# Which engine issues 120 stores of token sums in a decoder trunk's MLP

## The chip, the cores and the metric

The kernel runs on one core of a Trainium2 chip. The metric is the device time of one execution in microseconds (us), as the median of several runs. The core has a matrix engine (TensorE, PE in the profile, with its weight loads as PEld) and three engines for elementwise work: VectorE (DVE), ScalarE (ACT) and GpSimd (POOL). SyncE (SP) computes nothing here: its queue issues DMA transfers between on-chip memory and DRAM. Each engine works through its own list of instructions in order; a DMA is an instruction in the list of the engine that issues it, and the transfer then goes on by itself. Engines wait for each other, and for DMAs, through semaphores.

## What is computed

One layer of a decoder trunk for 2048 tokens of width 1024, in float32: a mixer (four retention heads beside a causal pooling mixer), cross-attention into 256 memory tokens, and a gated MLP, each behind an RMS norm and with a residual, and a last norm. The change lies in the MLP and in what prepares its operands:

```python
def conv_glu_ffn(h, w_up, conv_w, conv_b, w_down):
    a = h @ w_up                                  # 1024 -> 2 x 2816
    ...
    c = conv_w[0] * a2 + conv_w[1] * a1 + conv_w[2] * a + conv_b
    gate, val = jnp.split(c, 2, axis=-1)
    return (jax.nn.silu(gate) * val) @ w_down     # 2816 -> 1024
```

Here `a1` and `a2` are `a` shifted by one and two tokens.

## The kernel before

**Products.** Every float32 product is made from three matmul passes (L241 to L243): each operand is split in a high part and a low part, and high by high, high by low and low by high are added up. A high part is a copy (ACT, L955 for tokens, L1006 for weights), a low part is the difference (L216, on POOL or DVE). The MLP's two big products are done in blocks of two by two with seven block products in place of eight (the scheme of Strassen and Winograd). That needs, besides the blocks themselves, four sums of blocks on the weights' side and four on the tokens' side.

**Tokens' sums.** The tokens are held feature by token, as tiles of 128 features by 512 tokens (256 KB). They come in two blocks of 1024 tokens. Four tiles, two features by two halves of a block's tokens, give seven operand tiles. `sums_of` (L963) makes the four sums, all on POOL, in two steps: `t = b22 - b12`, `b12 = b11 - b12`, then `b11 = b11 + t`, `b21 = b11 - b21`. The seven tiles are written to DRAM, to `Hd` for the up product and to `Gd` for the down product: the originals as numbers 0, 3, 5 (and 7), the sums as 4, 1, 2 and 6. All these stores go through `send` (L972). `combining` (L944) loads an operand tile again later (`T<-Hd`, `T<-Gd`, L948) and splits it.

**Three places make them.** `first_tiles` (L1456) takes the first block's tiles, during the attention of the last block, near 1070 to 1120 us. It goes through four groups: load four tiles (`T<-Xd`, L1453), scale them (DVE, L225), sum, store, free. `later_tiles` (L1468) does the same with the second block's, step by step within the first block's up products (the first up round), at 1300 to 1380 us. Both use `normed_tiles` (L1429), with its store of the originals at L1438 and of the sums at L1445. For the down product, `Up.conv` makes a gated column of the up product's result; as soon as two columns that belong together are there, `pair` (L1099) loads the earlier one's tiles again (L1105, L1106), has POOL sum them with the later one's and stores the sums in `keep` (L1109). This happens 11 times in each of the two blocks.

**Places.** `T` is a set of ten places for tiles of 512 tokens (later re-cut to eleven, and two more named `state` and `consts` in the profile). Whatever takes a place waits until the last use of it is over, a store's landing included. `R` holds ten raw weight tiles, and seven pairs (`Q` and the end of `G`) hold split weights that wait for PE; `Z` holds the up product's results and gated columns, and the down product's sums.

**Order.** The Python code gives the program order by hand: `run` (L1324) walks over the products, a clock counts them, and `after(n, f)` puts a step n products later. From that order the framework's scheduler makes each engine's list with its own model of the instructions' times, so that a change of an instruction's engine can also shift instructions on other engines. An engine's list runs strictly in order: a store in SP's list that waits for POOL holds back the loads behind it.

**Weights' sums.** POOL issues DMAs already before the MLP: `weight_sums` (L903) adds blocks of the weights in DRAM by accumulating DMAs (`Ud<-w_up`, `Ud<-Ud` and the same for `Dd`, L915 to L922), 136 of them, between 47 and 936 us.

Of the kernel before, what the change touches and what calls it, by code (L numbers as in the profile page):

```python
# [21 lines left out]
SUB = 512  # L22
# [97 lines left out]
def trunk(ctx, tc, xT, memT, pos, w_qkgu, w_v, wkv, wqT, wo, wout_r, wout_p, poolT, w_up, w_dn, vecs, consts, outT):  # L120
    nc = tc.nc
    pe, act, dve, pool, sp = nc.tensor, nc.scalar, nc.vector, nc.gpsimd, nc.sync
# [42 lines left out]
    def cst(n):  # L165
        nonlocal o
        o += n
        return cs_t[:, o - n : o]

    ident, one = cst(P), cst(1)  # L170
# [8 lines left out]
    Hd = drp.tile([NB, KT // 2, 7, P, SUB], F32, tag="Hd", name="Hd")  # L179
# [7 lines left out]
    t = TT.take()  # L187
# [27 lines left out]
    def tt(eng, out, a, b, op):  # L215
        return eng.tensor_tensor(out=out, in0=a, in1=b, op=op)  # L216
# [7 lines left out]
    def stt(out, a, s, b, op0=ALU.mult, op1=ALU.add):  # L224
        dve.scalar_tensor_tensor(out=out, in0=a, scalar=s, in1=b, op0=op0, op1=op1)  # L225
# [737 lines left out]
    def sums_of(b11, b12, b21, b22, t):  # L963

        tt(pool, t, b22, b12, ALU.subtract)
        tt(pool, b12, b11, b12, ALU.subtract)
        yield
        tt(pool, b11, b11, t, ALU.add)
        tt(pool, b21, b11, b21, ALU.subtract)
        yield  # L970

    def send(to, aps):  # L972
        for i, a in aps.items():
            sp.dma_start(to[i], a)

    def in_turn(gens):

# [48 lines left out]
    class Up(Member):  # L1026
# [29 lines left out]
        def conv(self, g):  # L1056

            f = self.f + g * NF
            src = self.val if g else self.gate
            a = src.f[:, EDGE - 2 :]  # L1060

            def one():
                until_room(CC, 1)
                self.c[g] = CC.take()
                if self.b:
                    pool.tensor_copy(a[:, :2], halo[:, f])
                else:
                    pool.tensor_copy(halo[:, f], a[:, T:])
                act.activation(self.c[g].f, a[:, 2:], AF.Identity, bias=cb[:, f : f + 1], scale=cw[2][:, f : f + 1])  # L1069

            def two():
                c = self.c[g].f
                stt(c, a[:, 1 : T + 1], cw[1][:, f : f + 1], c)

            def three():
                c = self.c[g].f
                stt(c, a[:, :T], cw[0][:, f : f + 1], c)
                src.free()

            def four():  # L1080
                act.activation(self.c[0].f, self.c[0].f, AF.Silu)

            def five():
                tt(dve, self.c[1].f, self.c[1].f, self.c[0].f, ALU.mult)
                self.c[0].free()

                c = self.c[1]
                one, two = (c.f[:, h * SUB : (h + 1) * SUB] for h in ((1, 0) if self.b == NB - 1 else (0, 1)))
                at, second = halves[self.f]
                to = Gd[self.b, at]  # L1090

                def store():
                    send(to, {3: one, 5: two} if second else {0: one, 7: two})
                    if second:
                        pair()
                    else:
                        c.free()

                def pair():  # L1099
                    if TT.room() < 3:  # L1100
                        after(1, pair)
                        return
                    x = [TT.take() for _ in range(3)]
                    b11, b12, t = (r.f[:, :SUB] for r in x)
                    sp.dma_start(b12, to[7])  # L1105
                    sp.dma_start(b11, to[0])  # L1106
                    todo = sums_of(b11, b12, one, two, t)

                    def keep():  # L1109
                        send(to, {4: t, 1: b12, 2: b11, 6: one})  # L1110
                        for r in (*x, c):
                            r.free()

                    after(2, lambda: next(todo))
                    after(3, lambda: next(todo))
                    after(5, keep)

                after(2, store)

            return [one, two, three] + ([five] if g else [four])  # L1120
# [174 lines left out]
    def after(n, f):  # L1295

        waiting.append((clock[0] + n, f))

    def until_room(places, n):

        for _ in range(99):
            if places.room() >= n:
                return
            w = min(waiting, key=lambda w: w[0])
            waiting.remove(w)
            w[1]()
        assert False, "no room"
# [121 lines left out]
    def normed_tiles(b, j, q, rb):  # L1429

        for i, v in enumerate(q):
            n, s = j + 4 * (i // 2), i % 2
            stt(v, v, ffng[:, n : n + 1], rb[s].f[:, :SUB], ALU.mult, ALU.mult)
        if j == KT // 2 - 1:
            for r in rb:
                r.free()
        yield
        send(Hd[b, j], {0: q[0], 5: q[3], 3: q[2]})  # L1438
        t = TT.take()
        todo = sums_of(*q, t.f[:, :SUB])  # L1440
        next(todo)
        yield
        next(todo)
        yield
        send(Hd[b, j], {4: t.f[:, :SUB], 1: q[1], 2: q[0], 6: q[2]})  # L1445
        t.free()
        yield

# [7 lines left out]
    def first_tiles(own):  # L1456

        rb = [TT.take() for _ in range(NS)]
        spread(own[0], [r.f[:, :SUB] for r in rb], late=True)
        yield  # L1460
        for j in range(KT // 2):
            x = fetch_tiles(0, j)
            yield
            yield from normed_tiles(0, j, [r.f[:, :SUB] for r in x], rb)
            for r in x:
                r.free()

    def later_tiles(b, j, rb):  # L1468

        x = fetch_tiles(b, j)  # L1470
        steps = normed_tiles(b, j, [r.f[:, :SUB] for r in x], rb)

        def step():
            if next(steps, True) is None:
                after(2, step)
            else:
                for r in x:
                    r.free()

        after(2, step)  # L1480
# [246 lines left out]
```

## Time and profile before

| | |
|---|---|
| Runs shown | 2500.76, 2502.49, 2505.65 us |
| Median | 2502.49 us |
| The profiled execution | 2506.72 us (span of its instructions 2504.9 us, clock of PE 0.992 of full speed) |
| DMA, mean over the span | 474 MB, 189 GB/s |
| `T<-Xd` loads, by SP | 53 of 256 KB, 4.6 us to landing |
| `T<-Gd` loads, by SP | 168 of 256 KB, 4.1 us |
| SP waiting at a store for POOL (`T` and `Z`) | 67.6 + 17.5 us |

The profile is of one execution. Its page gives, for each engine, how long it was busy; a window gives the same for a stretch of time; a wait tells what an engine stood still for, in us in total, times and longest us. A group's row has the line of the code, the engine, the operation, output and input, then busy time and mean ns, and the idle time before it with what ended that. `POOL T L216` means: an instruction of POOL, of line 216, that writes `T`.

### The profile page before, as it was taken

To read this page: it belongs to the slowest core of one execution; us is meant where nothing else is said; L and a number is where in the kernel's file an instruction comes from. 1 tells how busy PE (TensorE), PEld (TensorE's weight loads), DVE (VectorE), ACT (ScalarE), POOL (GpSimd) and SP (SyncE) were. 2 spreads that over 40 slices of the span, in tenths; PEclk is the share of its full clock that TensorE was granted. 3 is DMA by queue.
4 is the path that set the end of the run, shared out by engine and by line. 5 is a ranking of instruction groups with operands and counts; after the bars stand their busy time and mean duration, and the time that the engine had idled before them with its cause. 6 is when DMAs were issued, how large, how long until landed. Compare 5 with 4: busy or idle time off the path is not lost.

```text
span 2504.9 us, 33172 instructions
## 1 busy us (share of the span) xinstructions
PE 2442.7 (98%) x11390; PEld 2037.7 (81%) x11390; DVE 1666.9 (67%) x2574; ACT 1216.1 (49%) x2163; POOL 652.4 (26%) x579
## 2 busy tenths in 40 slices
PE   6999999999999999999999999999999999999997
PEld 6888887788788888888887888878888887888885
DVE  8646566564635675574678776886677586867875
ACT  6333423343321223434654555665555576666663
POOL 1010122100121120030237352553335154222322
PEclk9999999999999999999999999999999999999998
DMA  8363888715766764366567564755556468768951
GB/s 318 89 168 110 244 191 233 234 40 181 227 152 145 159 158 149 111 221 220 167 205 270 166 203 153 236 192 165 160 160 213 136 220 287 250 185 280 346 164 68
DMA packets 257177, 474.28 MB, mean 189 GB/s; under 512 B 26864, under 2 KB 56176, under 8 KB 257008
## 3 DMA queue, kind: packets, MB, share of 16 engines
q1 hardware_dynamic: 212336, 408.18, 49.0%
q0 software_dynamic: 19584, 34.61, 8.9%
q10 hardware_dynamic: 25088, 29.37, 3.4%
q8 instruction: 89, 1.46, 0.2%
q14 instruction: 80, 0.66, 0.1%
HBM read 370.87 MB, written 170.39 MB: 216 GB/s over the span
## 4 chain that ended last, share of the span: by engine, by line
PE 78%; DMA 8%; DVE 6%; issue 3%; POOL 2%; ACT 2%; SPq 0%; POOLq 0%; ACTq 0%; DVEq 0%
PE mm L241 25%; PE mm L242 24%; PE mm L243 24%; POOL T L216 1%; DVE Z L216 1%; DMA T<-Xd 1%; DVE Z L225 1%; DVE G L216 1%; DMA T<-xT 1%; DVE Q L216 1%; DVE T L216 1%; DMA T<-Gd 1%; POOL Z L216 1%; PE aux L749 1%; DMA R<-VWd 0%
## 5 line engine op out<-in xcount | busy, mean ns | idle before, releaser
L241 PE MATMUL mm<-G,Q 128*128 128x512 f32 (+1 forms) x1888 | 728.1, 386 | 21.8 <-ACT Q L233 11.1
L243 PE MATMUL mm<-G,Q 128*128 128x512 f32 (+1 forms) x1888 | 725.9, 385 | 4.4 <-DVE Q L216 4.2
L242 PE MATMUL mm<-G,Q 128*128 128x512 f32 (+1 forms) x1888 | 725.7, 385 | 0.7 <-DVE G L216 0.7
L241 PE MATMUL mm<-G 128*128 128x512 f32 (+1 forms) x1380 | 532.1, 387 | 10.0 <-DVE Z L216 6.3
L242 PE MATMUL mm<-G 128*128 128x512 f32 (+1 forms) x1380 | 531.7, 386 | 0.0
L243 PE MATMUL mm<-G 128*128 128x512 f32 (+1 forms) x1380 | 531.1, 385 | 0.0
L241 PEld LDWEIGHTS mm<-G,Q 128*128 128x128 f32 x1888 | 357.8, 190 | 91.1 <-ACT Q L233 11.8
L243 PEld LDWEIGHTS mm<-G,Q 128*128 128x128 f32 x1888 | 357.7, 190 | 74.3 <-DVE Q L216 5.9
L242 PEld LDWEIGHTS mm<-G,Q 128*128 128x128 f32 x1888 | 358.0, 190 | 69.4 <-DVE G L216 1.6
L225 DVE SCALAR_TENSOR_TENSOR Z<-Z,vecs 128x1024 f32<-128x1024 f32 x176 | 276.3, 1572 | 153.5 <-ACT Z L1069 145.3
L241 PEld LDWEIGHTS mm<-G 128*128 128x128 f32 x1380 | 260.4, 189 | 64.5 <-DVE Z L216 8.0
L243 PEld LDWEIGHTS mm<-G 128*128 128x128 f32 x1380 | 260.2, 189 | 51.8
L242 PEld LDWEIGHTS mm<-G 128*128 128x128 f32 x1380 | 260.1, 188 | 51.5
L1006 ACT ACTIVATE G<-R 128x512 fp32r<-128x512 f32 (+1 forms) x272 | 166.5, 615 | 197.8 <-PE mm L242 178.6
L216 DVE TENSOR_TENSOR Z<-Z,mm 128x512 f32<-128x512 f32 x284 | 192.8, 679 | 78.2 <-PE mm L243 78.0
L216 DVE TENSOR_TENSOR Q<-R,Q 128x512 fp32r<-128x512 f32 x199 | 148.6, 748 | 143.4 <-ACT Q L233 138.9
L216 POOL TENSOR_TENSOR G<-R,G 128x512 fp32r<-128x512 f32 (+1 forms) x100 | 141.9, 1420 | 376.2 <-ACT G L1006 290.9
L233 ACT ACTIVATE Q<-R 128x512 fp32r<-128x512 f32 x150 | 93.8, 627 | 234.8 <-PE mm L242 187.3
L1006 ACT ACTIVATE Q<-R 128x512 fp32r<-128x512 f32 (+1 forms) x204 | 125.0, 613 | 90.9 <-PE mm L242 73.5
L216 DVE TENSOR_TENSOR G<-R,G 128x512 fp32r<-128x512 f32 (+1 forms) x168 | 131.5, 794 | 46.7 <-ACT G L233 38.0
L216 DVE TENSOR_TENSOR G<-T,G 128x512 fp32r<-128x512 f32 (+1 forms) x168 | 125.4, 758 | 53.9 <-ACT G L955 40.7
L940 ACT ACTIVATE aux<-R 128x512 f32<-128x512 f32 (+1 forms) x184 | 105.8, 576 | 95.8 <-DVE Q L216 52.9
(222 smaller groups left out, 2911.4 us busy)
## 6 DMA issues: line engine op xcount, KB each, us to landing
R<-Ud SPq DMA_DIRECT2D x176, 256.0 KB, 2.7
T<-Gd SPq DMA_DIRECT2D x168, 256.0 KB, 4.1
R<-w_up SPq DMA_DIRECT2D x132, 256.0 KB, 3.1
Gd<-Z SPq DMA_DIRECT2D x110, 256.0 KB, 2.4
Ud<-w_up SPq DMA_DIRECT2D x88, 256.0 KB, 5.9
R<-w_qkgu SPq DMA_DIRECT2D x32, 512.0 KB, 4.4
R<-Dd SPq DMA_DIRECT2D x64, 256.0 KB, 4.0
Gd<-T SPq DMA_DIRECT2D x56, 256.0 KB, 3.1
```

The costliest lines, as they stand in the source:

```text
L216: return eng.tensor_tensor(out=out, in0=a, in1=b, op=op)
L225: dve.scalar_tensor_tensor(out=out, in0=a, scalar=s, in1=b, op0=op0, op1=op1)
L233: act.activation(hi, src, AF.Copy)
L241: pe.matmul(ps, lh, rh, start=start, stop=False, skip_group_check=more)
L242: pe.matmul(ps, lh, rl, start=False, stop=False, skip_group_check=more)
L243: pe.matmul(ps, ll, rh, start=False, stop=stop, skip_group_check=more)
L749: pe.matmul(col(self.kv, c), col(self.kn.f, c), self.ch(v, c, h * T), start=True, stop=True)
L940: act.activation(t, x, AF.Copy)
L1006: act.activation(p2[:, 0, :w], self.raw[i].f[:, :w], AF.Copy)
```

## The change

`send` gets an argument that says which engine issues the stores, SP where nothing is given. The two calls that store the four sums pass POOL, the engine that has made them. The stores of the originals (0, 3, 5, 7) and all loads stay with SP. 32 stores to `Hd` and 88 to `Gd` change their engine.

```diff
-    def send(to, aps):
+    def send(to, aps, by=sp):
         for i, a in aps.items():
-            sp.dma_start(to[i], a)
+            by.dma_start(to[i], a)
...
                     def keep():
-                        send(to, {4: t, 1: b12, 2: b11, 6: one})
+                        send(to, {4: t, 1: b12, 2: b11, 6: one}, pool)
...
         next(todo)
         yield
-        send(Hd[b, j], {4: t.f[:, :SUB], 1: q[1], 2: q[0], 6: q[2]})
+        send(Hd[b, j], {4: t.f[:, :SUB], 1: q[1], 2: q[0], 6: q[2]}, pool)
         t.free()
```

## The prediction

> **What bounds the kernel now.** I read the page's busy times first.
>
> ```profile
> span 2504.9 us, 33172 instructions
> ...
> PE 2442.7 (98%) x11390; PEld 2037.7 (81%) x11390; DVE 1666.9 (67%) x2574; ACT 1216.1 (49%) x2163; POOL 652.4 (26%) x579
> ```
>
> PE is idle for 2504.9 − 2442.7 = 62 us in all, so only work that PE waits for, or comes to wait for, can move the time. The moved stores run between 1069 and about 2085 us. Next I read busy times by window there (columns: PE, PEld, DVE, ACT, POOL busy, then PE's clock, DMA share, GB/s), and the waits of PE in three stretches (1060 to 1130, 1290 to 1400, 2000 to 2120).
>
> ```profile
> 1060.00:1125.00 65.00, 64.80 (x307) 53.22 (x306) 47.21 (x85) 22.39 (x59) 22.41 (x17) 1.00 0.57 200
> 1290.00:1390.00 100.00, 94.20 (x406) 76.81 (x405) 79.12 (x77) 49.07 (x75) 67.23 (x47) 0.98 0.75 255
> ...
> 1350.00:1370.00 20.00, 16.81 (x69) 13.50 (x68) 17.04 (x15) 9.29 (x15) 16.28 (x12) 0.93 0.76 265
> 1700.00:1800.00 100.00, 100.00 (x443) 82.84 (x442) 67.05 (x67) 56.98 (x84) 40.27 (x34) 1.00 0.52 163
> 2050.00:2100.00 50.00, 46.69 (x200) 38.19 (x199) 35.22 (x41) 33.37 (x63) 24.79 (x18) 0.97 0.75 250
> ```
> ```profile
> PE aux L850 <- DVE T L220: 0.2, 1, 0.2
> ```
> ```profile
> PE mm L241 <- DVE Z L216: 5.8, 3, 3.2
> ```
> ```profile
> PE mm L241 <- ACT G L955: 3.3, 1, 3.3
> PE mm L241 <- DVE Z L216: 0.5, 1, 0.5
> ```
>
> So there are three places to price: the attention's end (PE full, POOL a third busy), a stretch of the MLP's first up round (1290 to 1390: POOL already busy 67 of 100 us, PE loses 5.8), and the passage from the up to the down products near 2080 (PE loses 3.3). In the steady stretch from 1700 PE has no gap.
>
> An idle us costs more than itself, since the clock dips after it: 443 matmuls in 100 us are 0.226 us each, so the 69 of 1350 to 1370 should take 15.6 us and took 16.81 beside 3.2 us idle, and the 200 of 2050 to 2100 should take 45.1 and took 46.69 beside 3.3. I charge 1.4 us for each us of new or removed idle time.
>
> **What the change moves.** 120 stores of 256 KB (32 to `Hd`, 88 to `Gd`) leave SP's queue and stand in POOL's stream behind the sums that make them. No byte and no sum is added. What a store costs on either side:
>
> ```profile
> Hd<-T SPq DMA_DIRECT2D x49, 256.0 KB, 2.4
> ...
> Ud<-Ud POOLq DMA_DIRECT2D x44, 256.0 KB, 6.1
> ```
> ```profile
> L974 SPq DMA_DIRECT2D Hd<-T x49: 319/320/752, 1069.0 to 1376.1; - x49
> ```
> ```profile
> L216 POOL TENSOR_TENSOR T<-T 128x512 f32<-128x512 f32 x57 | 88.8, 1559 | 170.8 <-DVE T L225 166.7 <-DMA Hd<-T 1.6
> ...
> L916 POOL DMA_DIRECT2D Ud<-w_up x22 | 21.5, 978 | 8.3 <-DMA Ud<-w_up 6.1 <-issue 1.9 <-DVE G L216 0.3
> L915 POOL DMA_DIRECT2D Ud<-w_up x22 | 19.8, 900 | 384.8 <-DMA Ud<-w_up 384.8
> L919 POOL DMA_DIRECT2D Ud<-Ud x22 | 18.3, 832 | 87.5 <-DMA Ud<-w_up 84.6 <-DVE sm L222 2.9
> ```
> ```profile
> L922 POOL DMA_DIRECT2D Ud<-Ud x22: 802/812/1127, 63.1 to 714.9; - x22
> ...
> DMA to landing us min/median/max: 3.7/5.3/7.4
> ```
>
> SP issues a store in 0.32 us. The trace has no plain store by POOL; its nearest row is the accumulating DMA of the same 256 KB, 0.8 to 1.0 us of POOL's own time. I take 0.85. In all that is 120 × 0.85 = 102 us more on POOL (26% becomes 30%), and 120 × 0.32 = 38 us less on SP. What PE sees of it is decided by who waits. The landing of a POOL store is not shown either. POOL's accumulates land in 5.3 us (they also read their target), SP's stores in 2.4. I take SP's 2.4 less its issue, 2.1, after POOL's issue: 2.95 us from its start. The ends are 2.0 and 5.3.
>
> *Attention's end.* The first block's four token tiles pass through `first_tiles` one after another: POOL's four sums, the store, then a load of the next tile into the place that the store has emptied, DVE's scaling (L225), the next sums. The waits of SP, the chain of waits and POOL's timeline show that ring:
>
> ```profile
> SPq L974 <- POOL T L216: 67.6, 65, 4.5
> ```
> ```profile
> 1089.52 4.66 DMA T<-Xd
> ...
> 1106.54 2.88 DMA T<-Xd
> ...
> 1110.64 2.67 DMA T<-Xd
> 1113.33 0.75 DVE T L225
> ```
> ```profile
> 1074.07 5.39 POOL L216 TENSOR_TENSOR T<-T 128x512 f32<-128x512 f32 x4 [137.09 <-DVE T L225]
> ...
> 1114.16 5.43 POOL L216 TENSOR_TENSOR T<-T 128x512 f32<-128x512 f32 x4 [9.67 <-DVE T L225]
> ```
> ```profile
> 1115.57 0.68 DVE L871 TENSOR_REDUCE sm<-mm 128x2 f32<-128x512 f32 x1
> ```
> ```profile
> 1119.89 0.41 PE L850 MATMUL aux<-consts,T 128*128 128x128 f32 x2 [0.20 <-DVE T L220]
> ```
>
> Three turns of the ring took 1114.16 − 1074.07 = 40.1 us. In the changed program POOL's order for a tile is sum, sum, store, sum, store, sum, store, store, and the loads of the next tile wait for the first three stores to land. One turn is then 5.4 (sums) + 2 × 0.85 (stores ahead of the third) + 2.95 (its landing) + 0.3 (SP's issue) + 3.4 (the load: mean of 4.66, 2.88 and 2.67) + 0.85 (L225 and the hand-over) = 14.6, three turns 43.8: the last L225 ends at 1117.8 instead of 1114.1. In DVE's new order it stands ahead of the last chunk's maximum (L871), which ran at 1115.57. That is 2.2 us late, and PE's transposes behind it (L850) had only 0.2 us to spare: +2.2. Behind PE the projection's matmuls stand in order, so nothing covers it. With stores landing in 2.0 and loads in 2.67 a turn is 12.9 and nothing is lost (0, and not below, as PE waits here for only 0.2); with 5.3 a turn is 17.0, three are 50.9, and PE loses 10.8 − 1.5 = 9.3.
>
> The Trainium skill (DMA: Bandwidth & Descriptors, Anatomy of one DMA) fits a POOL-issued transfer with 2.0 us plus the bytes over 436 GB/s, an estimate of 2.6 us for 256 KB, where POOL's own rows say 5.3. By it a turn would be 14.25 and the loss here 1.2 us in place of 2.2.
>
> *Second block's tiles, 1290 to 1390.* The same ring runs inside the up round, among POOL's pair sums. Its late loads reach PE through DVE, which waits in order for a tile (L225) while a finished product waits for it (`Z`, L216):
>
> ```profile
> DVE T L225 <- DMA T<-Xd: 12.5, 7, 5.7
> ...
> DVE state L225 <- DMA state<-Xd: 0.8, 1, 0.8
> ```
>
> Of these 13.3 us PE feels 5.8, or 44%. Each of the three later tiles now comes 2 × 0.85 + (2.95 − 2.4) = 2.25 us later, 6.75 together; by the same share PE loses 2.9. POOL carries 28 stores in this stretch (16 of tiles, 12 of three pairs): 67 + 24 = 91 of 100 us, full enough that I allow no gain from its own slack. Ends: −5.8 if SP, no longer held by stores, has the loads out in time, and +6.75 if all of it passes.
>
> *Passage at 2080.* PE waits for the first down tile:
>
> ```profile
> 2073.14 1.58 POOL Z L216
> 2074.74 0.32 SPq L974
> 2075.15 4.90 DMA T<-Gd
> 2080.07 0.64 ACT G L955
> ```
> ```profile
> 2080.78 1.28 POOL L216 TENSOR_TENSOR G<-T,G 128x512 fp32r<-128x512 f32 x1 [0.43 <-ACT G L955]
> ```
>
> Here the in-order queue costs something: the load at 2075.15 stood behind a store that waited for POOL. That store goes to POOL, and the first tile can come up to 2.2 us sooner. Against it, six stores and one sum less stand ahead of POOL's low half of the third tile: 6 × 0.85 − 1.25 = 3.85 us of POOL time, which ran without a gap. It would end at about 2085.9 in place of 2082.1. The profile shows no wait of PE for it, so it has an unknown reserve. I take +1.0, between −3.3 and +3.85.
>
> *Elsewhere* I take nothing: 1700 to 1800 has POOL at 40%, four more stores for each pair of halves make it about 50%, and the seven operand pairs made ahead (84 matmuls, 19 us) cover a run of four stores (3.4 us). If that cover were gone, a late low half would cost up to 3.4 us at each of some 20 pairs.
>
> Sum: 2.2 + 2.9 + 1.0 = 6.1, times 1.4 = +8.5 us. On the profiled execution's own 2506.72 that is 2515.2. That execution was 4.2 us above the median of the runs, so against 2502.49 it is **2511 us**. The sum's lower ends give (−5.8 − 3.3) × 1.4 = −13, the upper ones (9.3 + 6.75 + 3.85) × 1.4 = +28: 2490 to 2530.
>
> **The rivals.** *Faster: SP freed.* SP's queue no longer stands for 67.6 us behind POOL's sums, loads go out early, and the idle time at 1309 to 1370 and 2080 goes. For it: the load at 2075.15. Against it: in the token ring the loads wait for a place that only the store's landing frees, whoever issues it, and POOL lands it later. All of it would be −13; half, the more credible, 2496. It decides where the waiting store, not the place, held the load.
>
> *No change.* The 2.2 us at the attention's end fall into DVE's new order, the low half at 2080 has its reserve, and gain and loss inside 1290 to 1390 cancel: 2502. For it: PE is 98% busy with operands made ahead. Against: POOL at 91 of 100. The Trainium skill (DMA: Bandwidth & Descriptors, Issuing engines are not separate DMA queues) sides with it: issuing from another engine saves only the sequencer's time of starting the transfer.
>
> *Much slower: stores held up while DVE works.* If each POOL store took the longest issue and landing that its DMAs show (1.157 and 9.6 us), a turn at the attention's end would be 5.4 + 2.3 + 9.6 + 0.3 + 3.4 + 0.85 = 21.9: PE loses 24 there, about 2.9 + 3 × 7.3 × 0.44 = 12.5 in the second block, 1 at 2080: 37.5 × 1.4 = 53, or 2555 us.
>
> ```profile
> L915 POOL DMA_DIRECT2D Ud<-w_up x22: 807/813/1157, 47.7 to 699.7; - x22
> ...
> DMA to landing us min/median/max: 3.7/5.9/9.6
> ```
>
> Against it: the median of 0.81 us was had with DVE busy over half of the time. The Trainium skill (SBUF — State Buffer, Who interferes with whom) gives the mechanism: GpSimd writes the descriptors of its DMAs through ports that it shares with DVE, and is locked out while DVE runs a copy-like operation in its two-port mode.
>
> That the change doesn't do what it says is out: the built program has the 120 stores in POOL's stream.
>
> **How the numbers follow.** Likeliest, slower by the ring: 0.58 (2505 to 2528). Faster 0.18 (2490 to 2497), no change 0.16, much slower 0.08. 0.2% is 5 us, about what a measurement of this kernel tells from no change. A tenth of the likeliest falls inside that (0.06), a quarter of the no-change case outside it (0.02 on each side): faster 0.20, same 0.18, slower 0.62. The range of 8 in 10 leaves out the much slower case and the better half of the faster one: 2496 to 2530.
>
> **What would show it.** Right: POOL's rows hold 120 stores of 0.8 to 1.0 us; `first_tiles` begins its fourth tile about 4 us later after its first sum (43.8 in place of 40.1); PE waits about 2 us at L850 for DVE L220; the wait of L241 on `Z` between 1290 and 1400 grows from 5.8 to 8 or 9. Wrong: these waits shrink, PE comes to wait for POOL's low halves (L216 `G` or `Q`), or stores land in 6 us and more.

## The result, and the profile after

| | before | changed |
|---|---|---|
| Median | 2502.11 us (6 runs, 2500.76 to 2505.65) | 2518.62 us (6 runs, 2515.52 to 2520.02) |
| Ratio to before | | 1.0062, 95% interval 1.0051 to 1.0073 |
| The profiled execution | 2506.72 us | 2520.02 us |

The change makes the kernel 0.62% slower, some 15.5 us by the ratio. The page's busy times after:

```profile
span 2518.2 us, 33105 instructions
...
PE 2447.0 (97%) x11390; PEld 2037.3 (81%) x11390; DVE 1677.8 (67%) x2574; ACT 1216.9 (48%) x2163; POOL 688.0 (27%) x699
```

POOL is busy 36 us longer and has the 120 instructions more. DVE, for which nothing was changed, is busy 10.9 us longer (1666.9 before, 1669.5 in a second profile of before) over the same 2574 instructions. That is the first sign of something that the prediction did not have.

The store on its new engine, in the groups of one line (duration min/median/max in ns) and in the DMA issues (last column: us to landing):

```profile
L974 POOL DMA_DIRECT2D Gd<-T x56: 557/559/573, 1295.0 to 2097.7; - x56
L974 POOL DMA_DIRECT2D Hd<-T x28: 542/559/628, 1072.0 to 1390.0; - x28
```
```profile
Gd<-T POOLq DMA_DIRECT2D x56, 256.0 KB, 2.9
...
Hd<-T POOLq DMA_DIRECT2D x28, 256.0 KB, 3.9
Gd<-Z POOLq DMA_DIRECT2D x22, 256.0 KB, 4.5
```

A store takes 0.56 us of POOL, less than the accumulating DMAs (0.81). The 120 stores make 67 us, but POOL's total grew by only 36: its other work took some 31 us less than before, while DVE's took 11 more. The stores land 2.9 to 4.5 us after their issue. SP's groups before landed in 2.4 (`Hd<-T` and `Gd<-Z`, which hold originals too) and 3.1 (`Gd<-T`, sums alone). So the `Gd<-T` stores do not land later than SP's did; the others do, as far as the mixed groups tell.

What PE waits for, in the same three stretches as before (the last one to 2150, since the loss goes on), and two windows:

```profile
PE aux L850 <- DVE T L220: 2.0, 2, 1.1
```
```profile
PE mm L241 <- DVE Z L216: 10.5, 4, 5.7
```
```profile
PE mm L241 <- ACT Q L1006: 3.3, 2, 3.1
PE mm L241 <- ACT G L1006: 1.5, 1, 1.5
PE mm L241 <- ACT Z L1151: 0.8, 1, 0.8
PE mm L242 <- POOL G L216: 0.6, 1, 0.6
...
```
```profile
1290.00:1390.00 100.00, 90.67 (x388) 73.59 (x386) 76.94 (x70) 45.49 (x69) 73.72 (x73) 0.97 0.69 238
...
2050.00:2100.00 50.00, 45.41 (x187) 35.26 (x187) 37.32 (x41) 30.36 (x57) 28.35 (x25) 0.97 0.70 236
```

The waits that the prediction looked at have grown, or been replaced by others that add up to more (near 2080, 3.8 us before). To price the stages I took the start of every matmul from both traces (11390 in each) and subtracted by number, so that a stage's loss is the lag at its end less the lag at its start. All times are in us, against the first profile of before. The stages are named by their times there:

| kernel | before 1060 | attention's end | 1280 to 1420 | 1420 to 2000 | 2000 to 2160 | after 2160 |
|---|---|---|---|---|---|---|
| changed | -4.5 | +2.1 | +6.9 | +1.3 | +6.7 | +0.9 |
| changed, again (e12) | -3.9 | +1.5 | +5.7 | +4.0 | +7.5 | 0.0 |
| before, again (e11) | -6.3 | +0.9 | -1.4 | -2.7 | -0.7 | +0.9 |
| only Hd by POOL (e1) | -4.8 | +2.1 | +10.6 | -3.1 | -0.4 | 0.0 |
| only Gd by POOL (e2) | -4.5 | +1.7 | +2.5 | +0.4 | +6.7 | 0.0 |
| all by ACT (e3) | -6.9 | -0.4 | +6.0 | +1.4 | -1.8 | +0.9 |
| only first_tiles by POOL (e4) | -4.5 | +1.3 | +1.6 | -2.9 | +0.3 | 0.0 |
| POOL, stores behind the sums (e6) | -6.3 | +0.1 | +8.6 | +0.9 | +0.4 | +0.8 |
| Gd by POOL but the last 8 (e7) | +0.5 | +1.7 | +3.0 | +2.0 | +0.2 | +1.2 |
| POOL's time alone (e8) | -6.4 | -0.3 | +2.6 | -2.9 | +1.9 | +0.8 |
| last 8 by ACT (e10) | -7.3 | +1.5 | +0.1 | -2.9 | -1.9 | +1.8 |

Each row is one execution. The kernel of before differs from itself by up to 1.4 us in the three stages that were priced, by 2.7 between 1420 and 2000, and by 6 before 1060 us, where nothing was changed: its first profile had a 4.3 us wait there that all but e7's lack. At the attention's end the executions whose stores there were left with SP (e2, e7, e10, e11) show +0.9 to +1.7, those with POOL's stores there +0.1 to +2.1. So losses of 6 us are read from this table, losses of 2 us are not.

### The profile page after: what moved, and what is told of

It is laid out like the page before. It is cut to its first block, busy times and chain, and to the rows that moved or that the text cites. A ratio compares the mean times of both kernels' runs of the same rounds, so it can differ in the third digit from the quotient of the medians.

```text
span 2518.2 us, 33105 instructions
## 1 busy us (share of the span) xinstructions
PE 2447.0 (97%) x11390; PEld 2037.3 (81%) x11390; DVE 1677.8 (67%) x2574; ACT 1216.9 (48%) x2163; POOL 688.0 (27%) x699
## 4 chain that ended last, share of the span: by engine, by line
PE 46%; DVE 4%; DMA 3%; issue 2%; POOL 1%; ACT 1%; SPq 0%; POOLq 0%; DVEq 0%; ACTq 0%
PE mm L241 15%; PE mm L242 15%; PE mm L243 15%; DVE Z L225 1%; DMA T<-Xd 1%; DVE Z L216 1%; DVE G L216 1%; DMA T<-Gd 1%; POOL T L216 0%; POOL Z L216 0%; PE aux L242 0%; PE aux L241 0%; PE aux L243 0%; DMA Gd<-T 0%; DMA R<-Ud 0%
## 5 line engine op out<-in xcount | busy, mean ns | idle before, releaser
L241 PE MATMUL mm<-G 128*128 128x512 f32 (+1 forms) x1380 | 532.1, 387 | 16.8 <-DVE Z L216 10.5
L241 PEld LDWEIGHTS mm<-G 128*128 128x128 f32 x1380 | 260.1, 189 | 73.1 <-DVE Z L216 12.8
L1006 ACT ACTIVATE G<-R 128x512 fp32r<-128x512 f32 (+1 forms) x272 | 166.5, 615 | 193.7 <-PE mm L242 179.8
L216 POOL TENSOR_TENSOR G<-R,G 128x512 fp32r<-128x512 f32 (+1 forms) x100 | 136.7, 1369 | 364.3 <-ACT G L1006 290.5
L1006 ACT ACTIVATE Q<-R 128x512 fp32r<-128x512 f32 (+1 forms) x204 | 124.9, 613 | 86.8 <-PE mm L242 68.8
```

What stands on the lines that cost most here:

```text
L241: pe.matmul(ps, lh, rh, start=start, stop=False, skip_group_check=more)
L1006: act.activation(p2[:, 0, :w], self.raw[i].f[:, :w], AF.Copy)
```

## The experiments

**The parts.** e1 sends only the stores to `Hd` by POOL, e2 only those to `Gd`, e4 only the 16 of `first_tiles`:

```diff
-                        send(to, {4: t, 1: b12, 2: b11, 6: one}, pool)
+                        send(to, {4: t, 1: b12, 2: b11, 6: one})           # e1, e4
...
-        send(Hd[b, j], {4: t.f[:, :SUB], 1: q[1], 2: q[0], 6: q[2]}, pool)
+        send(Hd[b, j], {4: t.f[:, :SUB], 1: q[1], 2: q[0], 6: q[2]})       # e2
+        send(Hd[b, j], {4: t.f[:, :SUB], 1: q[1], 2: q[0], 6: q[2]}, pool if b == 0 else sp)   # e4
```

> Only the 32 stores to Hd (first_tiles and later_tiles) go to POOL, the 88 to Gd stay with SP. Theory A, each place pays for its own stores (attention's end +2.1 us, 1290 to 1400 +6.9 shared between tiles and pairs, 1640 to 1700 +1.3, 2050 to 2150 +6.7): about +6 us over before, 2508, with PE idle unchanged from before after 1600 us. Theory B, the scheduler's changed orders cost and not the stores: as the changed kernel, +12 us or more, with losses also after 1600 us. Theory C, the loss sits in the pairs' stores alone: within 2 us of before.

> Only the 88 stores to Gd go to POOL, the 32 to Hd stay with SP. Theory A: about +10 us, 2512: nothing at 1060 to 1130, some +3 between 1290 and 1400, and the whole loss at 1640 and 2050 to 2150. Theory B: as the changed kernel in all places. If the two parts add up, e1 and e2 together lose about 16 us.

> Only the 16 stores of first_tiles go to POOL. Theory A: +2 to +3.5 us, at 1112 to 1125 (PE waits about 2 us at L850 for DVE L220), nothing elsewhere. Theory B (orders): losses in the up round too, above +5 us.

Measured: e1 2510.54 us, 1.0042 (1.0027 to 1.0056); e2 2514.10, 1.0054 (1.0039 to 1.0069); e4 2504.18, 1.0008 (0.9997 to 1.0018), each against 2500.83. So the second block's tiles and the passage at 2080 pay for their own stores, as theory A had it: e1 loses nothing after 1420, and e2 has the whole loss of the passage. For the attention's end this is not shown: e2, which moved no store there, has +1.7 where nothing was expected, and e4 loses at most a few us in all. Theory B, that any new order costs, falls with e4, and theory C with e1. But the sizes were not theory A's (6 and 10 us), and the parts don't add up: 10.5 and 13.5 us are 24 together, and the changed kernel loses 15.5. Between 1280 and 1420 the tiles' stores alone (10.6) cost more than both kinds together (6.9 and 5.7).

The traces of the slower ones show where DVE's extra time is. Two stretches of the changed kernel, DVE's timeline first and POOL's under it (start, duration, instruction, in brackets the idle time before it), and the one of e1:

```profile
1306.56 3.53 DVE L225 SCALAR_TENSOR_TENSOR T<-T,vecs 128x512 f32<-128x512 f32 x1 [5.22 <-DMA T<-Xd]
```
```profile
1306.42 0.56 POOL L974 DMA_DIRECT2D Hd<-T  x1
1307.00 1.30 POOL L216 TENSOR_TENSOR Q<-R,Q 128x512 fp32r<-128x512 f32 x1
1308.24 1.29 POOL L216 TENSOR_TENSOR T<-consts,T 128x512 f32<-128x512 f32 x1
1309.48 0.56 POOL L974 DMA_DIRECT2D Hd<-consts  x1
```
```profile
2077.68 6.67 DVE L216 TENSOR_TENSOR G<-R,G 128x384 fp32r<-128x384 f32 x2
```
```profile
2078.85 0.56 POOL L974 DMA_DIRECT2D Gd<-consts  x1
2079.43 1.10 POOL L216 TENSOR_TENSOR T<-T,consts 128x512 f32<-128x512 f32 x1
2080.46 0.56 POOL L974 DMA_DIRECT2D Gd<-T  x1
2081.04 1.30 POOL L216 TENSOR_TENSOR T<-Z,T 128x512 f32<-128x512 f32 x1
2082.29 1.30 POOL L216 TENSOR_TENSOR Z<-T,Z 128x512 f32<-128x512 f32 x1
2083.52 0.56 POOL L974 DMA_DIRECT2D Gd<-T  x1
```
```profile
1356.42 6.99 DVE L225 SCALAR_TENSOR_TENSOR Z<-Z,vecs 128x1024 f32<-128x1024 f32 x1 [1.71 <-POOL T L216]
```

A scaling that takes 0.75 us elsewhere took 3.53, and ended when POOL's second store did. Of the two low halves at 2077.68, each 0.55 us when undisturbed, the second alone took 5.10 us (2079.25 to 2084.35), as long as POOL went from store to sum to store. In e1 one step of the convolution (1.27 us elsewhere) took 6.99. In both profiles of before no DVE operation of these kinds exceeds 2.34 us.

**DVE beside POOL, by itself.** e5 leaves out the trunk and runs DVE additions of 128x512 beside POOL:

> The trunk is left out; eight stretches one after another, in each of which DVE runs a chain of 12 additions of 128x512 beside POOL, and both meet at its end. POOL's part: (1) nothing, (2) a chain of 8 sums, (3) 8 stores of 256 KB, (4) sum and store in turn 8 times, (5) sum and memset of 128x512 in turn 8 times; with DVE's second input in PSUM instead of on-chip memory: (6) nothing, (7) sum and store in turn, (8) 8 sums. Theory L, a DVE operation of two on-chip inputs is held off for as long as POOL goes from sum to store to sum: 0.7 us each in (1), below 1.5 in (2), single ones of 3 us and more in (4), and none of that in (7). Theory O, POOL's time is all that a store costs: the longest DVE operation in (4) is no longer than in (2) and (5). If stores alone hold DVE off, (3) shows it too.

DVE's rows, in the order of stretches 1, 2, 3, 4, 5 and 7 (11 additions each):

```profile
6.14 8.89 DVE L170 TENSOR_TENSOR d<-d,c 128x512 f32<-128x512 f32 x11
...
17.64 15.47 DVE L170 TENSOR_TENSOR d<-d,c 128x512 f32<-128x512 f32 x11
...
35.72 8.90 DVE L170 TENSOR_TENSOR d<-d,c 128x512 f32<-128x512 f32 x11
...
47.22 18.42 DVE L170 TENSOR_TENSOR d<-d,c 128x512 f32<-128x512 f32 x11
...
68.24 13.60 DVE L170 TENSOR_TENSOR d<-d,c 128x512 f32<-128x512 f32 x11
...
98.63 7.91 DVE L176 TENSOR_TENSOR d<-d,ps 128x512 f32<-128x512 f32 x11
```

Alone an addition takes 0.69 us, beside POOL's sums 1.63, beside sum and memset 1.63 and 0.69 in turn, beside sum and store 2.11 to 2.13. Stores alone cost DVE nothing beyond the sum ahead of them (8.90 us as with one sum). With the second input in PSUM, sum and store cost nothing at all (0.69). So in these additions it is DVE's second input in on-chip memory that meets POOL (PSUM, where PE's results stand, is another memory), and a store between two sums makes it worse than sums alone: each of the six additions of 2.11 to 2.13 us began inside a store. The 3 us that theory L asked for were not reached: here each POOL sum waits for the one before it, and the profile shows 0.3 us of pause ahead of each store.

e9 takes these waits away, with a fixed order on POOL:

> The trunk is left out, as in the first such run, but POOL's instructions don't wait for each other: its order is fixed, and every one can start when the one before it is done, as POOL's sums, low halves and stores do in the trunk. DVE runs a chain of 16 additions of 128x512 (stretches 1 to 4) or 8 of 128x1024 (5 and 6). POOL: (1) 6 sums, (2) sum and store in turn, 6 times, (3) sum and memset in turn, (4) 6 stores, (5) sum and store in turn, (6) 6 sums. Theory L: in (2) and (5) one DVE addition lasts until POOL comes to a wait, 3 to 10 us; in (1), (3) and (6) none lasts longer than one sum more than its own time (1.6 and 2.4 us); in (4) 0.69 us throughout. If the long ones of the trunk have another cause, (2) shows 2.1 us as the chained sums did.

DVE in stretch 2, and POOL beside it:

```profile
28.01 5.92 DVE L173 TENSOR_TENSOR d<-d,c 128x512 f32<-128x512 f32 x2
```
```profile
29.04 0.69 POOL L156 DMA_DIRECT2D to<-c  x1
29.75 1.27 POOL L153 TENSOR_TENSOR p<-g,c 128x512 f32<-128x512 f32 x1
30.95 0.56 POOL L156 DMA_DIRECT2D to<-c  x1
31.54 1.27 POOL L153 TENSOR_TENSOR p<-g,c 128x512 f32<-128x512 f32 x1
32.74 0.56 POOL L156 DMA_DIRECT2D to<-c  x1
33.32 1.73 POOL L153 TENSOR_TENSOR p<-g,c 128x512 f32<-128x512 f32 x1
```

The first of the two additions took 1.63 us, the second 4.25: it began inside the first store and was held past two further sums, while POOL's sums kept their undisturbed 1.27. With sums alone the longest was 1.64, with sum and memset 1.65, with stores alone 1.63 and otherwise 0.69. So a store in POOL's stream is enough to hold DVE for several of POOL's instructions, with no trunk around it. It doesn't always: the later additions of that stretch took 1.63 to 1.78, and the wide ones of stretch 5 took 2.17, as beside sums alone. The moment of arrival seems to matter. In the six profiles of the changed kernel, e1, e2, e6 and e7, 20 DVE operations take over 2 us more than the shortest of their kind. Of these, 18 began while POOL was in a store, or within 0.01 us of its end, with POOL's next instruction right behind it. The other two, the 6.99 us one among them, began in a sum in e1. It is not settled: other operations began in a store and were not held.

The Trainium skill (SBUF — State Buffer, Who interferes with whom) says that a DVE instruction with two on-chip inputs and a GpSimd instruction that reads on-chip memory exclude each other for a whole instruction. The 0.69 and 1.63 us agree with that. That DVE can lose several turns in a row when stores stand between the sums goes beyond it.

**The store's place behind the sums, and POOL's time alone.** In e6 the four stores of a group are queued behind its fourth sum; e7 is e2 without the last two pairs' stores; in e8 SP stores as before, and POOL does small work instead, which adds nothing to the result:

```diff
+                        with tc.issue_after(made[0].ins):                  # e6: made[0] is the fourth sum
+                            send(to, {4: t, 1: b12, 2: b11, 6: one}, pool)
...
+                        send(to, {4: t, 1: b12, 2: b11, 6: one}, sp if self.b == NB - 1 and self.f >= NF - 2 else pool)   # e7
...
             sp.dma_start(to[i], a)                                         # e8
+            if extra:
+                pool.tensor_copy(phalo[:, 0, :2], a[:, :2])
+                for _ in range(4):
+                    pool.memset(phalo[:, 0, :2], 0.0)
```

> All 120 stores on POOL as in the changed kernel, but the four of a group are queued behind the group's fourth sum, so that POOL no longer alternates between store and sum. A group's first store leaves about 3 us later, its last at the same time. Theory L (DVE is held off while POOL goes from store to sum to store): the DVE operations of 3.5 to 7 us near 1306, 1356 and 2079 us are gone, the loss between 2050 and 2150 falls from 6.7 to 2 or less, and the whole comes to 2507 to 2511 in spite of later stores. Theory R (the ring: what costs is how late a store lands and its place comes free): it gets worse than the changed kernel, 2520 to 2526, most of it before 1400 us.

> As the one with only the Gd stores on POOL, but the 8 stores of the last two pairs, near 2070 us, stay with SP. If the loss of the Gd part sits in the passage from up to down (6.8 of 11.3 us in its profile), this comes to 2504 to 2508; if each of the 88 stores costs a little, it stays at 2512 to 2514.

> All stores by SP as before; in place of each of the 120 POOL does a copy of two columns and four tiny memsets (some 0.6 us of its time, no DMA). They add nothing to the result. Theory O, POOL's own time is what the stores cost: 2510 to 2520, losses in the places of the changed kernel. Theory L or R, the DMA itself matters (its descriptors beside DVE, its later landing): 2500 to 2507, and no DVE operation above 2.5 us.

Measured against 2500.85: e6 2508.53 us, 1.0038 (1.0025 to 1.0051); e7 2508.05, 1.0030 (1.0018 to 1.0042); e8 2504.19, 1.0017 (1.0008 to 1.0026).

e8 gives POOL more to do than the change does, and still loses only some 4 us:

```profile
PE 2441.1 (98%) x11390; PEld 2036.2 (81%) x11390; DVE 1670.4 (67%) x2574; ACT 1214.7 (49%) x2163; POOL 725.3 (29%) x1179
```

POOL's 725.3 us are 37 more than in the changed kernel. So POOL's own time makes about a quarter of the loss (2 to 6.5 us by the interval), and theory O falls as the main cause. e6 has the same 120 stores, at the same price, and gains back about 6 us of the 15.5 by their order alone (2 to 10, by the two intervals). Its loss at 2080 is 0.4 us instead of 6.7, the 5 us operation there is gone, and DVE's busy time is 1671.6 us instead of 1677.8. One operation of 3.5 us is left, near 1322. e7 shows the same from the other side: 8 stores fewer on POOL, and the loss at 2080 is 0.2. Over the eleven rows of the table, the loss of 6 us and more at 2080 and the 5 us operation stand together: in the two of the changed kernel and in e2, and nowhere else.

Between 1280 and 1420 e6 gains nothing (+8.6). There, the waits fit theory R: DVE's wait for a tile grows from 12.5 us before to 20.8 (1290 to 1400 in both; first row), and PE's from 5.8 to 12.2 (1290 to 1410). DVE's wait alone does not show it, though: it is 16.8 us in the changed kernel and 16.7 in e4, whose stores there are SP's and whose PE waits 6.0.

```profile
DVE T L225 <- DMA T<-Xd: 20.8, 3, 8.3
```
```profile
PE mm L241 <- DVE Z L216: 12.2, 4, 5.4
```

**Another engine.** e3 has ACT issue all 120, e10 only the 8 of the last two pairs, with SP issuing the rest as before:

```diff
-                        send(to, {4: t, 1: b12, 2: b11, 6: one}, pool)
+                        send(to, {4: t, 1: b12, 2: b11, 6: one}, act)      # e3, the Hd stores likewise
+                        send(to, {4: t, 1: b12, 2: b11, 6: one}, act if self.b == NB - 1 and self.f >= NF - 2 else sp)   # e10
```

> The same 120 stores are issued by ACT and by neither SP nor POOL. If what costs is POOL's time for a store (0.56 us, and what DVE suffers beside it) and the later landing (3.9 us against 2.4 for Hd), this is back at 2500 to 2506, and no DVE instruction of two on-chip inputs runs several times its usual time near 1306 and 2079 us. If taking the stores out of SP's order is what costs (loads that now run ahead of what PE needs first), it loses as much as the changed kernel, 2512 to 2520. ACT would then wait for POOL's sums, and PE for ACT (L1006, L955), which would be a loss of its own kind.

> All stores by SP as before, but the 8 of the last two pairs, near 2070 us, are issued by ACT, which has nothing to do there from 2072.5 to 2080 in the profile of before. If the first down tile's load stood behind a store in SP's queue there (the rival of the prediction, SP freed), PE's wait of 3.3 us near 2080 shrinks by 2 us or so and the kernel is 1 to 3 us faster than before: 2498 to 2500. If the place held it and not the queue, the same as before.

e3 measured 2507.23 us, 1.0031 (1.0017 to 1.0045), above the 2500 to 2506 that I expected. No DVE operation is held (longest 2.41 us), and nothing is lost at 2080. Its loss sits between 1280 and 1420 and is the other kind that the expectation named: ACT stands at a store that waits for POOL's sum, and PE waits for ACT to empty a result:

```profile
PE mm L241 <- DVE Z L216: 6.3, 4, 3.0
PE mm L241 <- ACT Z L1052: 5.9, 3, 2.6
```

e10 measured 2499.29 us against 2503.10, 0.9988 (0.9977 to 0.9999): 3 us faster than the kernel of before, at the edge of what can be told. Between 2000 and 2130 PE's wait for the down tile (last row) fell from 3.3 to 0.5 us, and its waits together from 3.8 to 2.4:

```profile
PE mm L241 <- DVE Z L216: 1.0, 1, 1.0
PE mm L241 <- ACT Z L1151: 0.9, 1, 0.9
PE mm L241 <- ACT G L955: 0.5, 1, 0.5
```

**Both kernels again**, for a second profile of each:

> The kernel of before once more, for a second profile to set the stages against. If the 2.1 us wait near 1656 us belongs to the kernel, it is there again; if it comes and goes from run to run, this profile goes without it like those of the variants that leave the Gd stores on SP, and is some 3 us shorter there. At the attention's end PE should wait no more than 0.2 us again.

> The changed kernel once more. The losses found in its first profile should be there again: about 2 us at the attention's end, 5 to 8 between 1290 and 1400, 5 to 7 between 2050 and 2150, and single DVE operations of 3 us and more, one of about 5 us near 2079.

e11 took 2497.28 us and e12 2521.37. In e12 the held operations came back, one of 5.10 us at 2080.53 and others of 3.1 to 3.9, and the losses with them (the table's second row), with 4.0 us between 1420 and 2000 that were not expected. In e11 the wait near 1656 was 1.3 us instead of 2.1, and PE waited 0.9 us at the attention's end, more than the 0.2 that I expected.

## Why the prediction was right, point by point

The direction and the range were right (2496 to 2530), the size was half: +8.5 us forecast, 15.5 measured (12.8 to 18.3). The later landings were forecast for the second block and are seen there. But a good part of the loss, some 6 us by e6, comes from held DVE operations, which the prediction did not have, and its attention's end is not shown to cost anything. That the sum still came out on the right side and in the range is in part luck.

- *Price of a store.* 0.85 us of POOL was taken from the accumulating DMAs; a plain store takes 0.56. The landing was put at 2.95 us with ends of 2.0 and 5.3; it is 2.9 for `Gd<-T`, 3.9 for `Hd<-T`, 4.5 for `Gd<-Z`. The price was too high, the landing of the `Hd` stores, on which the ring's sum rests, too low.
- *Attention's end, +2.2.* PE waits 2.0 us at L850 for DVE L220, as written, but not for the reason given. The three turns took 41.4 us, not 43.8:

```profile
1069.38 2.65 POOL L216 TENSOR_TENSOR T<-T 128x512 f32<-128x512 f32 x2 [136.64 <-DVE T L225]
...
1110.73 3.10 POOL L216 TENSOR_TENSOR T<-T 128x512 f32<-128x512 f32 x2 [6.60 <-DVE T L225]
```

  Set against PE's matmuls, the last chunk's maximum (L871) ran 0.35 us later than in before's first profile, and 0.2 earlier in e12, not 2.2 later. What makes PE wait are the two scalings behind it (L220), which run beside POOL's sums and stores. In the changed kernel, before and before's second profile:

```profile
1114.15 3.45 DVE L220 TENSOR_SCALAR T<-T,sm 128x256 f32<-128x256 f32 x2
```
```profile
1118.54 1.47 DVE L220 TENSOR_SCALAR T<-T,sm 128x256 f32<-128x256 f32 x2
```
```profile
1112.26 2.48 DVE L220 TENSOR_SCALAR T<-T,sm 128x256 f32<-128x256 f32 x2
```

  Such a scaling takes 0.34 us when undisturbed, and it varies in before too, where PE waited 0.2 and 0.9 us. With e4's 1.0008, whose interval holds 1, a price of this place is not shown: it lies between 0 and 2 us in the table, and the lateness of the ring makes at most 0.35 us of it.
- *Second block's tiles, +2.9, or 4.1 with the clock.* 6.9 and 5.7 measured. The waits fit the ring (e6, e1), and POOL's time may have some part (e8, +2.6, hardly more than the table can tell). What the term lacked is DVE itself: the tile's scaling, 0.75 us in the forecast, took 3.53 at 1306.
- *Passage at 2080, +1.0, or 1.4 with the clock.* This is the step that failed: 6.7 and 7.5. Both of its halves were about POOL's low half and the load behind SP's store. In the changed kernel's order the first down tile's load stood behind a weight load, which waited for a place of DVE's low half, the one that POOL held up:

```profile
SPq L1000 <- DVE G L216: 5.3, 2, 4.6
```
```profile
2084.38 0.33 SPq L1000
2084.81 2.75 DMA consts<-Gd
2087.58 0.64 ACT G L955
```

  ACT splits that tile and, next in its list, the weight for which PE then waits 3.1 us (`ACT Q L1006`). e6 and e7 show that with no such alternation there the loss is 0.2 to 0.4. The other half, that the load at 2075 stood behind a store in SP's order, was right: in e10, with ACT's stores, no DVE operation is held, and the first down tile's load goes out 2.9 us sooner, set against PE's matmuls. PE's waits there fall by 1.4 us.
- *Elsewhere, nothing.* +1.3 and +4.0 between 1420 and 2000, against 0 and -2.7 for before. Nearly all of it falls between 1640 and 1700. The five profiles that leave the `Gd` stores there with SP (e1, e4, e8, e10, e11) are at -2.7 to -3.1, the six that move them at +0.4 to +4.0, e3's with ACT's stores too; only before's first profile, at 0, stands between. So the moved `Gd` stores probably cost some 3 to 7 us here. Held DVE operations are not the whole reason, since e3 and e6 have none there. POOL is nearly full in the changed kernel, 19.07 of the 20 us from 1660 (10.89 before), but e3's POOL is not (9.95); the cause is left open. The steady stretch from 1700 to 1900, by whose first half the prediction judged the rest, lost nothing, as said.
- *The rivals.* "SP freed" was real, but shown at one place only, and worth some 3 us (0.3 to 5.8). "No change" fails. "Much slower: stores held up while DVE works" had the two engines right and the direction wrong: stores took 0.54 to 0.69 us whatever DVE did, and it was DVE that waited. POOL at 91 of 100 us in the second block came out at 74.

What is open: how the loss between 1280 and 1420 divides between later landings and held DVE operations (e1 alone loses more than the whole), what costs between 1640 and 1700, and what exactly lets POOL take several turns.

## What to carry to other kernels

Moving DMA issue to an engine that also computes had three prices here. Its own time was about a quarter of the loss. The transfer can land later for whoever waits for its place. And an engine that computes beside it can be held for several of its instructions. Look at the busy time of engines that the change doesn't touch: DVE's +10.9 us over the same instructions led to the held operations. In this kernel, moving a store that holds up an in-order queue gained something only at the place where a load behind it was late, and with an engine that was idle there.

## What was not expected of the hardware

- A DVE addition of two on-chip inputs, 0.69 us alone and 1.63 beside POOL's sums, took 4.25 us once when POOL went from store to sum without a pause. Held operations in the trunk took 3.1 to 7.0 us. In the small kernel POOL's sums then ran at 1.27 us, undisturbed. Memsets in place of the stores did not do that (1.65), nor did stores alone.
- A plain store costs POOL 0.56 us (0.54 to 0.63 in the changed kernel), nearly constant beside a busy DVE. An accumulating DMA of the same size has a median of 0.81, and single ones took up to 1.84.
